# A planner with durations from a trace, and two fine levels of hgrn2 as products of VectorE summed by GpSimd

## The chip, the cores and the metric

The kernel runs on one core of one Trainium2 chip. The metric is the device time of one execution in microseconds. Beside it stands, for one profiled execution, the span from its first to its last instruction.

## The reference, cut to what matters

A hybrid block of two layers over 272 tokens (16 learned "meta" tokens and 256 of the input; the reference pads to 384 positions, of which the first 112 are masked), D = 1024. In each layer three branches, retention, hgrn2 and differential attention, read one projection of the normed input, are gated, added and projected back, and a feed-forward part with a convolution over three tokens (width 2816) follows.

```python
proj = hn @ w_in                                    # 1024 -> 13312
branches = jnp.stack([retention(...), hgrn2(...), diff_attention(...)], axis=2)
y = jnp.sum(jax.nn.sigmoid(mg) * einsum('blnc,ncd->blnd', branches, w_branch), axis=2)
h = h + y @ w_out
h = h + conv_ffn(rms_norm(h, norm_ffn_g[li]), ...)  # in both layers
...
# hgrn2, for each of 8 heads of 128 features and each chunk of 128 tokens:
cb  = jnp.cumsum(lfc, axis=1)                       # log of the forget gates f
dec = exp(cb[:, :, None] - cb[:, None, :])          # for keys up to the query, else 0
a = jnp.einsum('bqhd,bkhd,bqkhd->bhqk', qc, kc, dec)
o = jnp.einsum('bhqk,bkhe->bqhe', a, vc) + jnp.einsum('bqhd,bhde->bqhe', qc * jnp.exp(cb), state)
```

The decay between a query and a key is a product of forget gates, another for each feature, so `a` isn't a plain matrix product.

## The kernel before, in words

**The stream of weights.** Activations lie with the features on the 128 partitions and the tokens along the free axis. The matrices come as chunks of eight tiles of 128 x 128 (`wraw`, three buffers; `_Weights.next`). ScalarE rounds a chunk to fp32r (`whi`, four buffers), VectorE takes the remainder (`wlo` = `wraw` - `whi`, four buffers), and TensorE issues three fp32r matmuls for a tile: `whi` with the high part of x (`xh`; L915), `whi` with its low part (`xl`; L916), `wlo` with the high part (L917). They sum into `main` in PSUM. A matmul has 272 columns (tokens), in layer 1 mostly 258. The last product of layer 1 has its own loop (`fo`, L1429 to L1431).

**The order.** `ORDER` lists the projections of a layer in turn (`hq`, `hf`, ..., each with its tile pair). Marks among them place the work of the branches: at `+hga` the first four heads of hgrn2 can begin, at `!hga` they must be done, `hgb` is the second four. `products` records the stream and moves a clock on; `behind` and `settle` spread the operations of a branch between its two marks, as due times (`key`).

Nothing is issued while it is recorded. Each call on an engine goes through `_Engine.__getattr__`, which adds an operation with a cost, its operands and the due time to `_Plan` (hence all these instructions have one line, L607). `_Plan.order` is a list scheduler: it simulates the five engines with these costs, and each time takes, on the engine that comes free first, the operation that can start earliest, by due time among equals. `issue` then writes the instructions in the order found. So a cost that is changed anywhere can move instructions on every engine. Each engine's own queue runs in order on the chip.

**hgrn2 by levels.** `hg_heads(b)` does four heads; it is called for b = 0 (`hga`) and 1 (`hgb`) in each layer, four calls in all. `q` (tile `hq`), `k` (tile `hf`) and `total` (tile `he`, the forget gates) are 128 x 4 heads x 272 tokens. The pairs of a query and a key within a chunk of 128 tokens are divided by `LEVELS` = 64, 32, ..., 2, 1: level s holds those whose key lies in the left and whose query in the right half of one block of 2s tokens. The levels go from 1 up to 64. After each, the queries of right halves are multiplied by the total decay of the left half, the keys of left halves by that of the right half, and the totals of two blocks are multiplied into one (`tot`, seven steps of falling width; both products show as `hq<-hq,tot` and `hf<-hf,tot`, at level 1 with `he`), so that at the next level the decays already stand in `q` and `k`.

The scores of levels 1 to 16 lie within blocks of 32 tokens. For each of them `quarters` issues 32 small matmuls (4 heads x 2 chunks x 4 blocks, 32 keys by 32 or 16 queries) into a PSUM bank `lev` (L1107; the trace has two rows for each), and VectorE copies the wanted elements under a mask into `near` (`copy_predicated`; partitions: keys). The call for level 1 also takes the diagonal, the call for level 2 also pairs that are apart by a key and an odd query, from queries that ScalarE gathers in `extra` (name `odd`).

```python
if s == 1:
    quarters(wide, q, lambda hd, c, t: q[:, hd, tokens(c, t)])
    dve.copy_predicated(near, lev[:, 80:112].unsqueeze(1).to_broadcast([P, 8, 32]), wide)
elif s < 32:
    quarters(some..., q, lambda hd, c, t: right(q[:, hd : hd + 1, tokens(c, t)], s)[:, 0])
    fill(right(near, s), lev[:, 16 * (i - 2) : 16 * (i - 1)], some)
```

`hg_outputs` later multiplies the scores (`at`, which takes `near`) with the values.

**GpSimd** (POOL in the profile) copies halves of words for transposing DMAs (`apart`, `vt`, `tails`), clears tiles, multiplies in the norms, and sums over the partitions for the heads' norms: `partition_all_reduce`, `hr<-hsq`, over 272 columns. In an order it shows as ISA; a nameless ISA row there loads the code of such an operation.

Of the kernel before, what the change touches and what calls it, by code (L numbers as in the profile page):

```python
# [25 lines left out]
T = META + SEQ  # L26
# [9 lines left out]
LEVELS = (64, 32, 16, 8, 4, 2, 1)  # L36
# [232 lines left out]
def _constants():  # L269
# [40 lines left out]
    block = [level(s, 32, 16) for s in LEVELS[2:6]] + [odd(32, 16), even(32, 32)]  # L310
    lev[:, :112] = np.tile(np.concatenate(block, axis=1), (4, 1))
# [45 lines left out]
class _Plan:  # L357
# [96 lines left out]
    def order(self):  # L454
# [13 lines left out]
        later = {e: [] for e in engines}  # L468
        now = {e: [] for e in engines}
        count = 0  # L470
        tables = "le"
        beside = False

        def push(op):
# [29 lines left out]
        while len(out) < todo:  # L504
# [69 lines left out]
class _Engine:  # L574
# [5 lines left out]
    def __getattr__(self, method):  # L580
        f = getattr(self.engine, method)

        def call(*args, **kw):
            aps = [(k, x) for k, x in list(enumerate(args)) + list(kw.items()) if isinstance(x, bass.AP)]
            outs = [x for k, x in aps if k in (0, "out", "accum_out")]
            ins = [x for k, x in aps if k not in (0, "out", "accum_out")]
            n = math.prod(outs[0].shape[1:])
            cost = self.fixed + self.each * n
            if self.name == "act":
                cost += 0.093 * (len(aps) - 2) - (0.043 if ins[0].tensor.name in self.plan.psum else 0.0)  # L590
            elif self.name == "pool" and method != "memset":
                cost += 1.6e-3 * n
            if method == "partition_all_reduce":
                cost = 0.4 + 5.4e-3 * n
            if method == "reciprocal":
                cost += 7 * self.each * n
            elif method == "tensor_tensor_scan":
                cost += self.each * n
            elif method == "transpose":
                cost = 0.11  # L600
            elif method == "matmul" and args[1].dtype == F32R:
                cost = max(0.107, n / 2400 + 0.003)
            elif method == "matmul":
                cost = max(0.214 if args[1].shape[-1] > 32 else 0.07, 4 * n / 2400)
            elif method == "dma_start":
                cost = self.fixed + self.each * n * outs[0].shape[0]
            self.plan.add(self.name, lambda: f(*args, **kw), cost, outs, ins, args[2] if method == "activation" else None)  # L607

        return call

# [55 lines left out]

def _trace(ctx, tc, plan, a, depth, probe):
    nc = tc.nc
    act = _Engine(plan, nc.scalar, "act", 0.094, 0.833e-3)
    dve = _Engine(plan, nc.vector, "dve", 0.068, 1.042e-3)  # L670
    pe = _Engine(plan, nc.tensor, "pe", 0.0, 4 / 2400)
    pool = _Engine(plan, nc.gpsimd, "pool", 0.04, 0.85e-3)
    sync = _Engine(plan, nc.sync, "sp", 0.06, 4 / 360e3)
# [20 lines left out]
    def slot(name, dt=F32):  # L694
        return new(sp, [P, 4 * T], dt, "slot", SLOTS, name)
# [13 lines left out]
    def bank(name):  # L709
        return new(bp, [P, 512], F32, "bank", 2, name)  # L710
# [4 lines left out]
    def tt(out, x, y, op):  # L715
        dve.tensor_tensor(out=out, in0=x, in1=y, op=op)
# [175 lines left out]
    def products(xs, name, j, t0=0):  # L892
# [96 lines left out]
    for li in range(depth):  # L989
# [74 lines left out]
        def hg_heads(b):  # L1064
# [28 lines left out]
            def right(t, s):  # L1093
                return halves(t, s, t.shape[2])[:, :, :, 1, :]
# [22 lines left out]
            extra = slot("extra")  # L1117
            odd = extra[:, : 8 * P].rearrange("p (h c t) -> p h c t", h=4, c=2)
            act.activation(qt2[:, :, 8:], right(q[:, :, tail], 1)[:, :, :, 0], AF.Copy)
            act.activation(odd[:, :, :, 64:], q[:, :, : 2 * P].rearrange("p h (c n two) -> p h c n two", c=2, two=2)[:, :, :, :, 1], AF.Copy)  # L1120
            tt(right(q, 1), right(q, 1), right(total, 1), MUL)
            room, at0 = slot("tot"), 0
            for i, s in reversed(list(enumerate(LEVELS))):

                pl = bank("lev")
                wide = pl[:, :256].rearrange("p (g t) -> p g t", g=8)
                some = pl[:, :128].rearrange("p (g t) -> p g t", g=8)
                tokens = lambda c, t: slice(c * P + 32 * t, c * P + 32 * t + 32)  # L1130
                if s == 1:
                    quarters(wide, q, lambda hd, c, t: q[:, hd, tokens(c, t)])
                    dve.copy_predicated(near, lev[:, 80:112].unsqueeze(1).to_broadcast([P, 8, 32]), wide)
                elif s == 2:
                    act.activation(odd[:, :, :, :64].rearrange("p h c (n s) -> p h c n s", s=2),
                                   q[:, :, : 2 * P].rearrange("p h (c n two s) -> p h c n two s", c=2, two=2, s=2)[:, :, :, :, 1, :], AF.Copy)
                    quarters(wide.rearrange("p g (two t) -> p g two t", two=2), odd,
                             lambda hd, c, t: odd[:, hd, c, :].rearrange("p (two t) -> p two t", two=2)[:, :, 16 * t : 16 * t + 16])
# [258 lines left out]
        def final():  # L1397
# [15 lines left out]
            cost = 3 * (BANK / 2400 + 0.012)  # L1413
# [216 lines left out]
```

## Time and profile before

| | before |
|---|---|
| time, median of 3 runs | 1305.88 us (1304.24 to 1306.25) |
| the profiled execution | 1305.7 us, span 1303.9 us |
| mean granted TensorE clock | 0.998 |
| PE, matmuls | busy 1285.8 us, 99% of the span, 11678 instructions |
| PE, weight loads (PEld) | 1256.7 us, 96% |
| DVE (VectorE) | 986.7 us, 76%, 1589 instructions |
| ACT (ScalarE) | 786.7 us, 60%, 1282 instructions |
| POOL (GpSimd) | 270.3 us, 21%, 300 instructions |
| DMA | 225 MB, mean 173 GB/s |

A busy time is the time in which an engine had an instruction under way, and the shares are those of the whole span. In the groups of instructions a row has line, engine, operation, out<-in, tile shapes and count, then busy time and mean ns of one, then the engine's idle time ahead of them and what ended most of it. In the waits a row says who waited, for whom, how long in sum, how often, and the longest. Rows that begin with a time are single instructions or batches: start (us), duration, engine, line, operation, and in brackets an idle time just before them with what ended it. Rows that begin with two times are stretches of the span: its length, busy time (and count) of PE, PEld, DVE, ACT and POOL, then the granted clock, the DMA share and GB/s.

### The profile page before, as it was taken

What the parts mean: (1) busy time and instruction counts of PE and PEld (TensorE: products, weight loads), DVE (VectorE), ACT (ScalarE), POOL (GpSimd) and SP (SyncE); (2) the same over time, 40 slices, a digit from 0 to 9 for tenths busy, and PEclk for the clock granted to TensorE, in tenths of its full rate; (3) what the DMA queues carried; (4) which work ended last, traced back from release to release, by engine and by line L of the source; (5) the groups of instructions that cost most, each with busy time, mean ns of one, the idle gap of its engine ahead of it and who ended that gap; (6) DMA issues with size and microseconds to landing.
All of it is one profiled execution on the core that took longest, in us unless ns stands there. A gap on an engine that the chain in (4) does not pass through costs nothing.

```text
span 1303.9 us, 28637 instructions
## 1 busy us (share of the span) xinstructions
PE 1285.8 (99%) x11678; PEld 1256.7 (96%) x11678; DVE 986.7 (76%) x1589; ACT 786.7 (60%) x1282; POOL 270.3 (21%) x300
## 2 busy tenths in 40 slices
PE   9999999999999999999999999999999999999998
PEld 9999989999999999999999999899999999999986
DVE  7685897798686789886575768877986867898843
ACT  6746444746576567666456474447466765776643
POOL 5021262423422020000030212634223220200000
PEclk9999999999999999999999999999999999999999
DMA  7664665643744545555555646655446446466653
GB/s 272 200 179 147 173 178 155 164 160 125 199 138 157 182 156 178 183 173 183 175 178 185 186 149 185 179 155 168 159 138 199 145 162 198 144 207 196 201 190 112
DMA packets 86868, 225.36 MB, mean 173 GB/s; under 512 B 32976, under 2 KB 33104, under 8 KB 86736
## 3 DMA queue, kind: packets, MB, share of 16 engines
q1 hardware_dynamic: 86448, 223.00, 55.3%
q8 instruction: 92, 1.51, 0.5%
q10 hardware_dynamic: 288, 0.52, 0.1%
q14 instruction: 40, 0.33, 0.1%
HBM read 216.16 MB, written 1.05 MB: 167 GB/s over the span
## 4 chain that ended last, share of the span: by engine, by line
PE 88%; DVE 9%; issue 1%; ACT 1%; DMA 0%; SPq 0%; DVEq 0%; ACTq 0%
PE main L915 26%; PE main L917 26%; PE main L916 25%; DVE wlo L607 2%; PE fo L1430 2%; PE fo L1431 2%; PE fo L1429 2%; DVE two_b L607 1%; DVE two_a L607 1%; PE lev L1107 1%; PE ds L1291 1%; PE ho L607 1%; PE ro L607 1%; PE do L607 1%; DVE two_c L607 1%
## 5 line engine op out<-in xcount | busy, mean ns | idle before, releaser
L915 PE MATMUL main<-xh,whi 128*128 128x272 f32 (+1 forms) x2368 | 682.6, 288 | 0.8 <-ACT whi L607 0.8
L917 PE MATMUL main<-xh,wlo 128*128 128x272 f32 (+1 forms) x2368 | 673.9, 285 | 1.3 <-DVE wlo L607 0.7
L916 PE MATMUL main<-xl,whi 128*128 128x272 f32 (+1 forms) x2368 | 673.3, 284 | 1.5 <-DVE xl L607 1.5
L607 DVE TENSOR_TENSOR wlo<-wraw,whi 128x1024 fp32r<-128x1024 f32 (+1 forms) x411 | 512.0, 1250 | 187.8 <-ACT whi L607 186.6
L607 ACT ACTIVATE whi<-wraw 128x1024 fp32r<-128x1024 f32 (+1 forms) x411 | 427.5, 1042 | 250.9 <-PE main L916 166.3
L917 PEld LDWEIGHTS main<-xh,wlo 128*128 128x128 f32 x2368 | 446.5, 189 | 3.1 <-DVE wlo L607 2.3
L916 PEld LDWEIGHTS main<-xl,whi 128*128 128x128 f32 x2368 | 446.6, 189 | 2.2 <-DVE xl L607 1.9
L915 PEld LDWEIGHTS main<-xh,whi 128*128 128x128 f32 x2368 | 446.7, 189 | 2.0 <-ACT whi L607 1.0
L607 POOL TENSOR_TENSOR y<-h,rstd 128x272 f32<-128x272 f32 x32 | 34.6, 1112 | 318.1 <-ACT rstd L607 318.1
L607 POOL PARTITION_ALL_REDUCE hr<-hsq x36 | 65.8, 1837 | 88.9 <-ACT hsq L607 85.9
L607 DVE SCALAR_TENSOR_TENSOR two_b<-main,small,two_b 128x256 f32<-128x256 f32 (+2 forms) x144 | 65.3, 487 | 24.4 <-ACT two_b L607 22.7
L607 POOL COPY apart<-vsrc 128x512 uint16<-128x512 uint16 x48 | 40.7, 867 | 145.2 <-ACT vsrc L607 145.0
L607 ACT ACTIVATE two_b<-main,small 128x272 f32<-128x272 f32 (+1 forms) x72 | 37.3, 566 | 23.8 <-PE main L917 22.7
L915 PE MATMUL main<-ghi,whi 128*128 128x272 f32 x176 | 51.0, 290 | 0.0
L916 PE MATMUL main<-glo,whi 128*128 128x272 f32 x176 | 50.6, 287 | 0.0
L917 PE MATMUL main<-ghi,wlo 128*128 128x272 f32 x176 | 50.3, 286 | 0.0
L607 POOL COPY vt<-turned 128x512 uint16<-128x512 uint16 x32 | 37.0, 1160 | 29.2 <-DMA turned<-apart 29.0
L915 PE MATMUL main<-b0hi,whi 128*128 128x272 f32 (+1 forms) x128 | 37.9, 296 | 0.0
L915 PE MATMUL main<-b1hi,whi 128*128 128x272 f32 (+1 forms) x128 | 37.8, 296 | 0.0
L915 PE MATMUL main<-yhi,whi 128*128 128x272 f32 (+1 forms) x128 | 36.4, 284 | 0.0
L917 PE MATMUL main<-b0hi,wlo 128*128 128x272 f32 (+1 forms) x128 | 36.4, 284 | 0.0
L917 PE MATMUL main<-yhi,wlo 128*128 128x272 f32 (+1 forms) x128 | 36.3, 284 | 0.0
(235 smaller groups left out, 1970.1 us busy)
## 6 DMA issues: line engine op xcount, KB each, us to landing
wraw<-in_w SPq DMA_DIRECT2D x402, 512.0 KB, 3.4
h<-in_h SPq DMA_DIRECT2D x4, 272.0 KB, 5.1
dec<-in_dec SPq DMA_DIRECT2D x2, 544.0 KB, 4.9
wraw<-in_w SPq DMA_DIRECT2D x4, 256.0 KB, 4.2
const<-in_const SPq DMA_DIRECT2D x1, 937.0 KB, 5.6
turned<-apart SPq DMA_TRANSPOSE x48, 4.0
gain<-in_gl SPq DMA_DIRECT2D x1, 512.0 KB, 5.1
out<-y ACTq DMA_DIRECT2D x2, 256.0 KB, 2.8
```

Of the source, the lines that this page charges most:

```text
L607: self.plan.add(self.name, lambda: f(*args, **kw), cost, outs, ins, args[2] if method == "activation" else None)
L915: nc.tensor.matmul(o, wh, hi, start=first, stop=False)
L916: nc.tensor.matmul(o, wh, lo, start=False, stop=False)
L917: nc.tensor.matmul(o, wl, hi, start=False, stop=last)
L1107: nc.tensor.matmul(o, keys, x, start=True, stop=True)
L1291: nc.tensor.matmul(ss[m][:, at : at + nk], q[half, hd, q0 : q0 + P], k[half, hd, :nk], start=True, stop=True)
L1429: nc.tensor.matmul(o, gh, wh, start=False, stop=False)
L1430: nc.tensor.matmul(o, gl, wh, start=False, stop=False)
L1431: nc.tensor.matmul(o, gh, wl, start=False, stop=end)
```

## The change

It has two parts.

**The planner's costs.** ScalarE's and VectorE's fixed costs go up (0.094 to 0.2 us, 0.068 to 0.145), a main matmul's from 0.003 to 0.01 us over its columns, GpSimd's operations get costs of their own, a transposing DMA 0.7 us more. New is `RELOAD`: where GpSimd goes from a `tensor_tensor` to a `partition_all_reduce` or back, the plan adds 8 us.

**Levels 1 and 2 of `hg_heads`.** Instead of the groups of small matmuls VectorE forms products of a query and a key elementwise (128 features x all tokens of four heads), GpSimd sums them over the 128 partitions (`sums`: in pieces of 544 columns, five in a call), and VectorE copies from the sums in SBUF, 32 partitions at a time since each block of 32 tokens has its place there. `mine` is a query with its own key at odd tokens (before the decays), `prod` (1088 columns) both queries of a pair with the left key, and at level 2 the two queries of a right half with each of the two left keys (two halves of 544). ScalarE's two gathering copies are gone. There are two new slots of a shared pool, `prod` and `sums`, and the mask table has some other columns.

```diff
 class _Plan:
+    RELOAD = 8.0
...
+            if e == "pool" and op.func is not None:
+                if op.func != code:
+                    code, t = op.func, max(t, engines[e] + self.RELOAD)
...
+            elif self.name == "pool" and method == "tensor_tensor":
+                cost, kind = 0.55 + 2.1e-3 * n, method
+            elif method == "partition_all_reduce":
+                cost, kind = 0.2 + 6.3e-3 * n, method
...
-    act = _Engine(plan, nc.scalar, "act", 0.094, 0.833e-3)
-    dve = _Engine(plan, nc.vector, "dve", 0.068, 1.042e-3)
+    act = _Engine(plan, nc.scalar, "act", 0.2, 0.833e-3)
+    dve = _Engine(plan, nc.vector, "dve", 0.145, 1.052e-3)
...
-        cost = 3 * ((T - t0) / 2400 + 0.003)
+        cost = 3 * ((T - t0) / 2400 + 0.01)
...
+            def sums(out, prod):
+                for c in range(0, prod.shape[1], 2 * T):
+                    pool.partition_all_reduce(out[:, c : c + 2 * T], prod[:, c : c + 2 * T], P, ReduceOp.add)
...
-            act.activation(odd[:, :, :, 64:], q[...][:, :, :, :, 1], AF.Copy)
+            tt(mine, rows(q, 2)[:, :, 1], rows(k, 2)[:, :, 1], MUL)
+            sums(own, mine)
             tt(right(q, 1), right(q, 1), right(total, 1), MUL)
+            tt(prod.rearrange("p (n s) -> p n s", s=2), rows(q, 2), rows(k, 2)[:, :, 0:1].to_broadcast([P, 2 * T, 2]), MUL)
+            sums(total_of, prod)
+            for t, here in lanes():
+                dve.copy_predicated(blocks_of[here], lev[here, 80:112]..., by_chunk(total_of, P)[here, :, :, here])
+            for t, here in lanes():
+                dve.copy_predicated(blocks_of[here]...[:, :, :, :, 1], lev[here, 64:80]..., by_chunk(own, P // 2)[here, ...])
...
                 if s == 1:
-                    quarters(wide, q, lambda hd, c, t: q[:, hd, tokens(c, t)])
-                    dve.copy_predicated(near, lev[:, 80:112]..., wide)
+                    pass
                 elif s == 2:
-                    act.activation(odd[:, :, :, :64]..., q[...][:, :, :, :, 1, :], AF.Copy)
-                    quarters(wide..., odd, ...)
-                    fill(right(near, 2), lev[:, 48:64], wide[:, :, :16])
-                    fill(right(near, 1), lev[:, 64:80], wide[:, :, 16:])
+                    for kk, x in enumerate(halves_):
+                        tt(x.rearrange("p (n s) -> p n s", s=2), rows(q, 4)[:, :, 2:], rows(k, 4)[:, :, kk : kk + 1]..., MUL)
+                    sums(total_of, prod)
+                    for t, here in lanes():
+                        for kk, c in enumerate((48, 112)):
+                            dve.copy_predicated(to, split_s(mask), split_s(data))
```

The names in the rows that follow are tiles with a running number; the number tells which chunk or call a row belongs to.

VectorE in the second call of layer 0 (`hgb`), between the chunks `wlo_406` and `wlo_453`: `near_266` collects the scores, `hq_101_254` and `hf_44_149` are the call's queries and keys, `tot` its totals, `prod_268` the new products, `sums_269` and `extra_267` what GpSimd has summed. Before:

```order
L607 TENSOR_TENSOR wlo_406<-wraw_404,whi_405 128x1024
L607 COPY_PREDICATED near_266<-masks_80,lev_271 128x32x4
L607 TENSOR_TENSOR hq_101_254<-hq_101_254,tot_268 128x136x4
L607 TENSOR_TENSOR hf_44_149<-hf_44_149,tot_268 128x136x4
L607 TENSOR_TENSOR wlo_453<-wraw_451,whi_452 128x1024
```

And after:

```order
L615 TENSOR_TENSOR wlo_406<-wraw_404,whi_405 128x1024
L615 COPY_PREDICATED near_266<-masks_80,sums_269 32x256 x4
L615 COPY_PREDICATED near_266<-masks_80,extra_267 32x128 x4
L615 TENSOR_TENSOR prod_268<-hq_101_254,hf_44_149 128x544
L615 TENSOR_TENSOR hq_101_254<-hq_101_254,tot_270 128x272x2
L615 TENSOR_TENSOR hf_44_149<-hf_44_149,tot_270 128x272x2
L615 TENSOR_TENSOR wlo_453<-wraw_451,whi_452 128x1024
```

Three rows between two chunks became eleven, eight of them copies out of SBUF; the chain stands a level earlier at this place (level 2's decays, where level 4's stood).

VectorE in the first call of layer 0 (`hga`), behind `wlo_294`. Before:

```order
L607 TENSOR_TENSOR wlo_294<-wraw_292,whi_293 128x1024
L607 TENSOR_TENSOR hf_38_131<-hf_38_131,tot_217 128x4x8x16
L607 TENSOR_TENSOR hq_36_123<-hq_36_123,tot_217 128x4x8x16
L607 COPY_PREDICATED near_215<-masks_80,lev_222 128x8x16
L607 TENSOR_TENSOR wlo_298<-wraw_296,whi_297 128x1024
```

After (between the two pieces stand the other six `tot_219` steps, another `prod_217`, and level 2's `hf` and `hq`):

```order
L615 TENSOR_TENSOR wlo_294<-wraw_292,whi_293 128x1024
L615 TENSOR_TENSOR prod_217<-hq_36_123,hf_38_131 128x544
L615 TENSOR_TENSOR tot_219<-he_139 128x544
```
```order
L615 COPY_PREDICATED near_215<-masks_80,sums_218 32x256 x4
L615 COPY_PREDICATED near_215<-masks_80,extra_216 32x128 x2
L615 TENSOR_TENSOR hf_38_131<-hf_38_131,tot_219 128x136x4
L615 TENSOR_TENSOR hq_36_123<-hq_36_123,tot_219 128x136x4
L615 COPY_PREDICATED near_215<-masks_80,extra_216 32x128 x2
L615 TENSOR_TENSOR wlo_298<-wraw_296,whi_297 128x1024
```

Behind `wlo_294` the chain of levels was nearly done before; now it is at level 2, and 21 rows stand ahead of `wlo_298` instead of three.

GpSimd in that first call, ahead of the heads' norms (`hr<-hsq`). Before:

```order
L607 COPY vt_194<-turned_208 128x2x256 x2
L607 MEMSET am_265 128x64
L607 MEMSET near_266 128x256
L607 ISA
L607 ISA hr_233<-hsq_232 128x272
```

After:

```order
L615 COPY tails_195<-vsrc_196 128x32
L615 ISA
L615 ISA extra_216<-extra_216 128x544
L615 COPY vt_194<-turned_198 128x2x256 x2
L615 ISA sums_218<-prod_217 128x544 x2
L615 COPY apart_207<-vsrc_206 128x512 x2
L615 COPY tails_195<-vsrc_206 128x32
L615 MEMSET am_265 128x64
L615 ISA sums_218<-prod_217 128x544 x2
```

The code is loaded once, as before, but ahead of the sum of `mine`; five sums over 544 columns stand among the copies for the values.

TensorE in `hgb` of layer 0: where the first group of small matmuls stands in the stream (`main_380`, `main_400` and `main_450` are PSUM tiles of the stream). Before:

```order
L917 MATMUL main_380<-xh_16_91,wlo_383 128x272
L1107 MATMUL lev_269<-hq_101_254,hf_44_149 32x32 x32
L915 MATMUL main_380<-xh_16_91,whi_382 128x272
```

After:

```order
L925 MATMUL main_400<-xh_14_89,wlo_406 128x272
L1115 MATMUL lev_271<-hq_101_254,hf_44_149 32x16 x32
L615 MATMUL s_175_418<-rq_316,rk_333 128x272
L923 MATMUL main_450<-xh_16_91,whi_452 128x272
```

The first group of this call is now that of level 4 and stands five chunks later. Over the whole program TensorE has 576 calls of `lev` matmuls instead of 832 (1152 rows of the trace instead of 1664).

More of the change, by code (lines that the diff above doesn't have):

```diff
@@ L470, in order @@
         count = 0
-        tables = "le"
+        tables, code = "le", "tensor_tensor"
         beside = False
@@ L605, in call @@
             elif method == "dma_start":
-                cost = self.fixed + self.each * n * outs[0].shape[0]
-            self.plan.add(self.name, lambda: f(*args, **kw), cost, outs, ins, args[2] if method == "activation" else None)
+                cost = self.fixed + self.each * n * outs[0].shape[0] + (0.7 if kw.get("transpose") else 0.0)
+            self.plan.add(self.name, lambda: f(*args, **kw), cost, outs, ins, kind)
         return call
@@ L1119, in hg_heads, with by_chunk @@
+            def by_chunk(t, n):
+                return t.rearrange("p (h x) -> p h x", h=4)[:, :, : 2 * n].rearrange("p h (c x) -> p h c x", c=2)
+            extra, prod, total_of = slot("extra"), slot("prod"), slot("sums")
+            mine, own = extra[:, : 2 * T], extra[:, 2 * T :]
+            rows = lambda t, n: t.rearrange("p h (n s) -> p (h n) s", s=n)
             act.activation(qt2[:, :, 8:], right(q[:, :, tail], 1)[:, :, :, 0], AF.Copy)
-            act.activation(odd[:, :, :, 64:], q[:, :, : 2 * P].rearrange("p h (c n two) -> p h c n two", c=2, two=2)[:, :, :, :, 1], AF.Copy)
+            tt(mine, rows(q, 2)[:, :, 1], rows(k, 2)[:, :, 1], MUL)
@@ L1121, in hg_heads @@
+            sums(own, mine)
             tt(right(q, 1), right(q, 1), right(total, 1), MUL)
+            tt(prod.rearrange("p (n s) -> p n s", s=2), rows(q, 2), rows(k, 2)[:, :, 0:1].to_broadcast([P, 2 * T, 2]), MUL)
+            sums(total_of, prod)
+            blocks_of = near.rearrange("p (h c) t -> p h c t", c=2)
+            for t, here in lanes():
+                dve.copy_predicated(blocks_of[here], lev[here, 80:112].unsqueeze(1).unsqueeze(1).to_broadcast([32, 4, 2, 32]),
+                                    by_chunk(total_of, P)[here, :, :, here])
@@ L1122, in hg_heads @@
+            for t, here in lanes():
+                dve.copy_predicated(blocks_of[here].rearrange("p h c (n two) -> p h c n two", two=2)[:, :, :, :, 1],
+                                    lev[here, 64:80].unsqueeze(1).unsqueeze(1).to_broadcast([32, 4, 2, 16]),
+                                    by_chunk(own, P // 2)[here, :, :, 16 * t : 16 * t + 16])
             room, at0 = slot("tot"), 0
             for i, s in reversed(list(enumerate(LEVELS))):
-                pl = bank("lev")
-                wide = pl[:, :256].rearrange("p (g t) -> p g t", g=8)
@@ L1129, in hg_heads @@
-                some = pl[:, :128].rearrange("p (g t) -> p g t", g=8)
+                pl = bank("lev") if s > 2 else None
+                some = s > 2 and pl[:, :128].rearrange("p (g t) -> p g t", g=8)
                 tokens = lambda c, t: slice(c * P + 32 * t, c * P + 32 * t + 32)
                 if s == 1:
-                    quarters(wide, q, lambda hd, c, t: q[:, hd, tokens(c, t)])
-                    dve.copy_predicated(near, lev[:, 80:112].unsqueeze(1).to_broadcast([P, 8, 32]), wide)
+                    pass
@@ L1412, in final @@
                     pe.matmul(accs[t][k // 4][:, k % 4 * P : (k % 4 + 1) * P], h[:, k, tokens(t)], ident, is_transpose=True, start=k % 4 == 0, stop=False)
-            cost = 3 * (BANK / 2400 + 0.012)
+            cost = 3 * (BANK / 2400 + 0.0133)
             groups = [(t, c) for t in range(2) for c in range(2)]
```

36 lines of the change are left out of this document (19 added, 17 removed).

## The prediction

> **What bounds the kernel now.** I read the page first, then the waits, then stretches of the timeline.
>
> ```profile
> PE 1285.8 (99%) x11678; PEld 1256.7 (96%) x11678; DVE 986.7 (76%) x1589; ACT 786.7 (60%) x1282; POOL 270.3 (21%) x300
> PE 88%; DVE 9%; issue 1%; ACT 1%; DMA 0%; SPq 0%; DVEq 0%; ACTq 0%
> ```
>
> PE is the bound: it is never idle for long, and the chain that ended last runs through its weight stream. So a microsecond taken off PE's own work is a microsecond of the kernel, and so is each one for which PE has to wait. DVE, busy 76% on average, is off the path as long as its `wlo` tiles come in time. How much time it has is seen in the waits.
>
> ```profile
> DVE wlo L607 <- ACT whi L607: 186.6, 171, 4.7
> ACT whi L607 <- PE main L916: 166.3, 134, 2.9
> PE lev L1107 <- DVE hf L607: 3.2, 2, 1.7
> PE lev L1107 <- DVE tot L607: 0.4, 1, 0.4
> ```
>
> ACT waits for PE to free a `whi` buffer, DVE then for ACT: the split of the weights runs as far ahead as its four buffers let it, and no further. The small last rows are PE waiting for the hgrn2 chain. Here are the instructions that set the pace of both.
>
> ```profile
> 80.05 0.28 PE L917 MATMUL main<-xh,wlo 128*128 128x272 f32 x1
> 80.27 0.76 PE L1107 MATMUL lev<-hq,hf 128*32 128x32 f32 x64
> 80.96 0.40 PE L915 MATMUL main<-xh,whi 128*128 128x272 f32 x1
> 81.20 0.29 PE L916 MATMUL main<-xl,whi 128*128 128x272 f32 x1
> 81.33 0.29 PE L917 MATMUL main<-xh,wlo 128*128 128x272 f32 x1
> L607 ACT ACTIVATE whi<-wraw 128x1024 fp32r<-128x1024 f32 x399 | 421.4, 1057 | 246.1 <-PE main L916 163.2 <-PE fo L1430 26.5 <-DMA wraw<-in_w 26.3
> L607 DVE TENSOR_TENSOR wlo<-wraw,whi 128x1024 fp32r<-128x1024 f32 x399 | 504.3, 1268 | 184.2 <-ACT whi L607 183.1
> ```
>
> A main matmul starts 0.123 us after the one before (81.20 to 81.33 is 0.13, and the long stretches agree), so a chunk of eight weight tiles, 24 matmuls, lasts 2.95 us on PE. `whi` of a chunk can begin when PE is done with the chunk four before it, three chunks (8.85 us) ahead of its own use; less 1.06 for `whi`, 1.22 for an undisturbed `wlo` and some 0.3 for the handovers, a `wlo` is ready at most 6.2 us ahead. That lead is all that hides a burst of other work on DVE.
>
> **The change part by part.**
>
> *PE loses the 32-call groups of the two finest levels*, eight of them (two in each of four `hg_heads`). The rows from 80.05 to 81.33 span 1.28 us where three main matmuls would take 0.37: a group costs 0.91. **-7.3 us**, wholly on the path.
>
> *PE's waits in `lev`*: the two rows above are 3.6 us, and I take them as gone, since those groups now stand later: **-3.6**. One of them left more behind:
>
> ```profile
> 829.00:833.00 4.00, 2.30 (x75) 2.11 (x75) 3.96 (x7) 1.75 (x4) 3.96 (x5) 1.00 0.76 244
> 833.00:836.00 3.00, 3.00 (x40) 2.97 (x29) 3.00 (x5) 1.43 (x3) 1.06 (x1) 0.63 0.41 115
> 836.00:839.00 3.00, 3.00 (x79) 2.82 (x78) 1.16 (x3) 0.00 (x0) 0.54 (x1) 0.81 0.73 180
> ```
>
> PE idled 1.7 us before 833, and then the granted clock (third number from the end) was 0.63 and 0.81 for 3 us each: 1.1 + 0.6 = 1.7 us lost. **-1.7**, if the wait goes.
>
> *DVE gains work.* One call now has these rows more or dearer:
>
> ```profile
> L607 DVE TENSOR_TENSOR hf<-hf,tot 128x544 f32<-128x544 f32 x12 | 10.7, 894 | 0.2 <-PE lev L1107 0.2
> L607 DVE TENSOR_TENSOR hq<-hq,he 128x1088 f32<-128x1088 f32 x4 | 6.4, 1607 | 0.0
> L607 DVE COPY_PREDICATED near<-masks,lev 128x128 f32<-128x128 uint8 x20 | 7.0, 352 | 2.3 <-PE lev L1107 2.1
> L607 DVE COPY_PREDICATED near<-masks,lev 128x256 f32<-128x256 uint8 x4 | 1.8, 444 | 0.0
> L607 DVE TENSOR_TENSOR tot<-he 128x544 f32<-128x544 f32 x4 | 3.3, 818 | 0.0
> L607 DVE TENSOR_TENSOR tot<-tot 128x272 f32<-128x272 f32 x4 | 2.1, 516 | 0.1
> L607 DVE TENSOR_TENSOR tot<-tot 128x136 f32<-128x136 f32 x4 | 1.5, 373 | 0.1
> L607 DVE TENSOR_TENSOR tot<-tot 128x68 f32<-128x68 f32 x4 | 1.8, 448 | 0.1
> L607 DVE TENSOR_TENSOR tot<-tot 128x32 f32<-128x32 f32 x4 | 1.3, 335 | 0.1
> L607 DVE TENSOR_SCALAR he<-he,keep,floor 128x272 f32<-128x272 f32 x16 | 7.8, 518 | 0.0
> L607 DVE TENSOR_SCALAR hf<-hf,keep 128x272 f32<-128x272 f32 x16 | 7.6, 497 | 0.0
> ```
>
> Products: three of 544 elements (0.9 each) and one of 1088 (1.6), 4.3 us. Copies on 32 partitions: four of 256 elements (0.44) and twelve of 128 (0.35), 6.0; that a copy on a quarter of the partitions takes as long as one on all is my assumption, and the highest value. Gone are one of 256 and two of 128, 1.1. Net 9.2 us a call, 37 in all. Spread over 1304 us this would vanish; what counts is where it stands. I take the stretch in the second call of layer 0 (`hgb`), from the end of `wlo_386` to the end of `wlo_453`, five chunks later.
>
> After, DVE's rows there are seven TENSOR_TENSOR of 544 (6.3), two of 1088 (3.2), the first five `tot` steps (0.82 + 0.52 + 0.37 + 0.45 + 0.34 = 2.5), four copies of 256 and four of 128 (3.2) and five `wlo` (6.1): 21.3 us. Before, the same stretch held 17.5 (six of 544, one of 1088, `tot` of 544, 272, 136, 68, 32 and 16, one copy of 256, three of 128, five `wlo`). PE takes 5 x 2.95 = 14.75 us for the five chunks; before, four and a half `lev` groups stood among them (4.1); now all of these lie behind. `wlo_386` itself comes behind four `he` and four `hf` steps (4.1) and two short ones (0.9, both sides have them), so its lead is 6.2 + 2.95 - 4.1 - 0.9 - 1.2 = 2.95, and 4 if the `he` steps overlap as usual; I take 4. So the time to hand was 14.75 + 4.1 + 4 = 22.9 for 17.5, with 5 us to spare, and is now 18.8 for 21.3: **PE waits 2.5 us**. Layer 1 has the same rows between the same two `wlo`: another 2.5.
>
> In the first call (`hga`) the rows bunch instead: between `wlo_294` and `wlo_298` stand 11.7 us (six of 544, seven `tot` steps for 3.2, four and four copies) against 0.9 before. `wlo_298` ends 11.7 + 1.2 = 12.9 after `wlo_294`; it may take the lead of 6.2, a chunk of 2.95 and the `lev` group and transpose that follow (1.0), 10.2: a wait of 2.7. In layer 1 the bunch is 7.7 + 1.2 against 4.6 + 2.95 + 2.0 = 9.6: none. Sum of these waits: **+7.7**.
>
> *GpSimd gains 20 sums over 544 columns, and they hold DVE.* This is the cost that the plan doesn't know.
>
> ```profile
> 112.86 1.23 DVE L607 TENSOR_TENSOR wlo<-wraw,whi 128x1024 fp32r<-128x1024 f32 x1 [2.93 <-ACT whi L607]
> 114.90 3.79 POOL L607 PARTITION_ALL_REDUCE hr<-hsq  x2 [12.26 <-ACT hsq L607]
> 116.82 2.23 DVE L607 TENSOR_TENSOR wlo<-wraw,whi 128x1024 fp32r<-128x1024 f32 x1 [2.41 <-ACT whi L607]
> 158.06 1.88 POOL L607 PARTITION_ALL_REDUCE hr<-hsq  x1
> 159.70 1.22 DVE L607 TENSOR_TENSOR wlo<-wraw,whi 128x1024 fp32r<-128x1024 f32 x1 [1.69 <-ACT whi L607]
> ```
>
> The second sum of the pair began about 116.8. The `wlo` that began with it took 2.23 us instead of 1.23; the one that began in the last 0.24 us of a sum took 1.22. So the first part of a sum over 272 columns keeps an operation with two SBUF inputs waiting for 1.0 us. For 544 columns I estimate 2.0 (if it goes by columns; 1.0 if it goes by instructions) and a sum of 3.7. Nearly all of DVE's rows in the stretch above read two SBUF tiles, and DVE has no idle time there, so each of a call's five sums can add 0 (it falls on other rows) to 2.0 us: 0 to 10 for each `hgb`, 0 to 4 for `hga` of layer 0, 0 to 3.4 for `hga` of layer 1 (0.6 to spare), since there the first sums meet DVE with time to hand. I take three of five in `hgb` (6 + 6), one in `hga` of layer 0 (2) and 1 for layer 1: **+15**, of 0 to 27. Behind every wait stands a `wlo` in DVE's queue, and behind that PE.
>
> The Trainium skill ("GPSIMD Engine Reference", Specifications) states this contention for DVE instructions with two SBUF inputs or in a 2-port mode. By it the masked copies, which no row here shows beside a sum, would be held as well; the sum would then stand 4 us higher.
>
> *The cold clock again*: by the rows at 829 to 839, a wait of 1.7 us can cost another 1.7. Four places now wait longer than that, 6.8 us; a slower PE gives DVE time to catch up, so I count half: **+3.4**, of 0 to 6.8.
>
> The Trainium skill ("TensorE: Matmul & The Clock Gate", Part 1) has the clock halved only after about 3.4 us of idleness. The drop here came after 1.7, so the measurement decides; by the page the waits, which come in pieces, would leave the clock alone, and the forecast would be 3.4 lower.
>
> *At nothing*: ACT loses eight copies (busy 60%). GpSimd's change of code, the nameless row ahead of its first sum, was hidden before (that sum began 0.13 us after its `hsq`); now it stands right ahead of the first `extra` sum, but DVE asks for the result only behind `wlo_294`, some 18 us later, and the sums and copies between take 9.3: up to 9 us are covered, and the nearest row bounds it by the 12.3 us that GpSimd idled ahead of 114.90, so +3 at worst. *The new order elsewhere* (attention heads, feed-forward) I take at 0, -3 to +3: PE's other waits in the list are small.
>
> Sum: -7.3 - 3.6 - 1.7 + 7.7 + 15 + 3.4 = **+13.5 us**. The profiled execution took 1305.7 (its span is 1303.9), the median of the three runs is 1305.88: **1319 us**.
>
> **The rivals.** A measurement of this kernel can tell about 0.2% (2.6 us) from no change.
>
> *Faster, 20%*: the sums meet DVE while it waits or reads PSUM, and costs of copies are lower on 32 partitions. For it speaks that in most of the trace a `wlo` beside GpSimd takes its usual 1.22. Without any hold and cold clock: -12.6 + 7.7 = -4.9, 1301; if the leads cover the bunches too, -12.6, 1293. It decides where the waits added stay below 10 us.
>
> *No change that can be told, 12%*: the waits added come to 10 to 15 us.
>
> *Much slower, 18%*: every sum holds DVE for its 2 us, in all four calls: +27 instead of +15, with a cold clock each time: +29, 1335. GpSimd's own lateness would show here too: DVE's second product waits for GpSimd to have read the first, with the next `wlo` behind it.
>
> *Likeliest, 50%*: as summed.
>
> **How the numbers follow.** The forecast is 1319. The low end takes the hold-free case with a little of the bunching, 1298; the high end the full hold, 1335. Faster by over 0.2%: 0.20, within: 0.12, slower: 0.68 (0.50 + 0.18).
>
> **What the profile after would show.** Right: the `lev` rows of PE fall from 1664 to 1152; PE's idle time grows by some 15 to 20 us, ended by DVE `wlo` or `near`, near 105 us, 175 to 190 us and the same places of layer 1; the sums over 544 columns take 3.4 to 4 us; DVE's 544 rows beside them take 2 us longer; several dips of the granted clock. Wrong: PE without new waits at these places, or waits elsewhere.

## The result

The changed kernel took 1353.63 us (median of 4 runs, 1350.37 to 1354.72) against 1305.75 of the kernel before on the same chip: 47.9 us slower, a ratio of 1.036 (95% interval 1.0343 to 1.0377). The forecast was 13.5 us slower: it had the sign, and the hold of VectorE as its largest term, but little more than a quarter of the size.

The page of the changed kernel, first the engines, then the chain that ended last by engine:

```profile
PE 1296.6 (96%) x11166; PEld 1266.1 (94%) x11166; DVE 1066.6 (79%) x1657; ACT 777.0 (57%) x1270; POOL 346.3 (26%) x320
PE 74%; DVE 18%; issue 2%; DMA 2%; ACT 2%; POOL 2%; SPq 0%; DVEq 0%; ACTq 0%; POOLq 0%
```

The span is 1351.8 us, the mean granted clock 0.985 (before 1303.9 and 0.998). TensorE has 512 instructions less, as planned, and yet is busy 10.8 us longer. It is idle 55.2 us (1351.8 - 1296.6) where it was idle 18.1: 37.1 more. Both together are the 47.9. VectorE has doubled its share of the chain.

What TensorE waited for in the changed kernel (in all, times, longest):

```profile
PE main L925 <- DVE wlo L615: 17.9, 9, 7.1
PE lev L1115 <- DVE hq L615: 11.7, 4, 4.9
PE lev L1115 <- DVE hf L615: 6.7, 2, 3.8
```

The longest of these waits begins at 183 us, in `hgb` of layer 0. VectorE and GpSimd there, in order of time:

```profile
179.10 3.93 POOL L615 PARTITION_ALL_REDUCE extra<-extra  x1 [1.82 <-DVE extra L615]
179.80 3.36 DVE L615 TENSOR_TENSOR prod<-hq,hf 128x1088 f32<-128x1088 f32 x1
183.26 0.73 DVE L615 TENSOR_TENSOR hf<-hf,he 128x544 f32<-128x544 f32 x1
183.32 7.33 POOL L615 PARTITION_ALL_REDUCE sums<-prod  x2 [0.29 <-DVE prod L615]
183.90 3.47 DVE L615 TENSOR_TENSOR hq<-hq,he 128x1088 f32<-128x1088 f32 x1
187.30 5.08 DVE L615 TENSOR_TENSOR wlo<-wraw,whi 128x1024 fp32r<-128x1024 f32 x2
```

Three sums stand nearly back to back, and whatever VectorE issues within the first two microseconds of one gets to work only when that part is over: the product of 1088 takes 3.36 us and `hq` 3.47 (the shortest rows of these kinds take 1.6 and 1.3), and the two `wlo` 5.08 where two undisturbed ones take 2.4. The row of 544 that had begun 0.06 us before a sum kept its 0.73; there the sum became longer instead (3.9 us instead of 3.5). TensorE needs the first `wlo` from 183.6 on. In stretches of 3 us (length, then busy time and count of PE, PEld, DVE, ACT, POOL, then the granted clock, DMA share, GB/s):

```profile
180.00:183.00 3.00, 3.00 (x27) 3.00 (x26) 3.00 (x1) 0.06 (x1) 3.00 (x1) 1.00 0.32 124
183.00:186.00 3.00, 0.62 (x5) 0.40 (x4) 2.90 (x3) 1.20 (x2) 2.71 (x2) 1.00 0.00 0
186.00:189.00 3.00, 0.00 (x0) 0.00 (x0) 3.00 (x2) 0.74 (x2) 3.00 (x2) 0.69 0.00 0
189.00:192.00 3.00, 1.24 (x5) 1.24 (x6) 3.00 (x2) 0.00 (x0) 3.00 (x3) 0.50 0.16 22
192.00:195.00 3.00, 3.00 (x19) 3.00 (x18) 3.00 (x4) 0.00 (x0) 3.00 (x4) 0.68 0.78 235
195.00:198.00 3.00, 3.00 (x26) 3.00 (x25) 2.82 (x6) 1.96 (x2) 0.70 (x1) 1.00 0.70 273
```

TensorE stood from 183.6 to 190.8. The clock fell to half at about 187.1 (0.69 over 186 to 189) and was full again at 193.9 (0.68 over 192 to 195), so the first 3.2 us of work after the wait ran at half speed.

### The profile page after: what moved, and what is told of

It is laid out like the page before. It is cut to its first block, busy times and chain, and to the rows that moved or that the text cites. A ratio compares the mean times of both kernels' runs of the same rounds, so it can differ in the third digit from the quotient of the medians.

```text
span 1351.8 us, 27644 instructions
## 1 busy us (share of the span) xinstructions
PE 1296.6 (96%) x11166; PEld 1266.1 (94%) x11166; DVE 1066.6 (79%) x1657; ACT 777.0 (57%) x1270; POOL 346.3 (26%) x320
## 4 chain that ended last, share of the span: by engine, by line
PE 74%; DVE 18%; issue 2%; DMA 2%; ACT 2%; POOL 2%; SPq 0%; DVEq 0%; ACTq 0%; POOLq 0%
PE main L923 22%; PE main L925 21%; PE main L924 21%; DVE wlo L615 6%; DVE near L615 2%; DMA wraw<-in_w 2%; DVE hq L615 2%; PE fo L1467 1%; PE fo L1465 1%; PE fo L1466 1%; DVE hf L615 1%; DVE two_c L615 1%; ACT whi L615 1%; PE ds L1327 1%; DVE prod L615 1%
## 5 line engine op out<-in xcount | busy, mean ns | idle before, releaser
L615 DVE TENSOR_TENSOR wlo<-wraw,whi 128x1024 fp32r<-128x1024 f32 (+1 forms) x411 | 526.1, 1290 | 163.3 <-ACT whi L615 162.2
L925 PEld LDWEIGHTS main<-xh,wlo 128*128 128x128 f32 x2368 | 451.2, 191 | 18.7 <-DVE wlo L615 18.7
L924 PEld LDWEIGHTS main<-xl,whi 128*128 128x128 f32 x2368 | 451.7, 191 | 4.3 <-DVE xl L615 3.9
L923 PEld LDWEIGHTS main<-xh,whi 128*128 128x128 f32 x2368 | 452.2, 191 | 2.3 <-PE main L925 0.8
L615 POOL PARTITION_ALL_REDUCE hr<-hsq x36 | 73.0, 2043 | 101.0 <-ACT hsq L615 101.0
L615 POOL PARTITION_ALL_REDUCE sums<-prod x16 | 58.8, 3709 | 21.8 <-DVE near L615 19.2
L923 PE MATMUL main<-yhi,whi 128*128 128x272 f32 (+1 forms) x128 | 36.4, 284 | 0.0
L925 PE MATMUL main<-yhi,wlo 128*128 128x272 f32 (+1 forms) x128 | 36.4, 284 | 0.0
```

The costliest lines, as they stand in the source:

```text
L923: nc.tensor.matmul(o, wh, hi, start=first, stop=False)
L924: nc.tensor.matmul(o, wh, lo, start=False, stop=False)
L925: nc.tensor.matmul(o, wl, hi, start=False, stop=last)
```

## The experiments

Four theories. A: each sum over 544 columns holds VectorE for about 2 us, wherever it meets it. B: VectorE waits for what GpSimd has summed. C: the new order itself costs the time. D: VectorE's products and copies alone are too much. How long VectorE was held is counted in all runs in one way: of each VectorE row that overlaps a partition sum, what it took beyond the shortest row of its form. In the changed kernel that comes to 41.3 us beside the 20 sums, 2.06 each, and none of the four calls is spared.

**The new costs alone**, with the levels as before (`_Plan`, `_Engine` and the two matmul costs of the change, `hg_heads` and the masks of before).

> New planner costs with the old levels (small matmuls, copies from PSUM), so no sum over 544 columns. Theory A (each sum over 544 columns holds VectorE for about 2.1 us, VectorE falls behind with wlo, TensorE waits and its clock falls): the loss is not in the planner; 1300 to 1312 us. Theory C (the new order itself costs the time): 1335 us or more. TensorE's waits of over 0.5 us sum to 10 to 20 us by A, to 40 by C.

1315.21 us, a ratio of 1.0079 (1.0064 to 1.0094): 10.4 us slower. So neither A nor C alone: some of the loss comes with the costs, but not most. New among TensorE's waits is one for GpSimd's `tails`:

```profile
PE vm L614 <- POOL tails L614: 6.2, 3, 2.5
PE lev L1114 <- DVE hf L614: 4.6, 3, 2.2
```

**Which of the costs.** Two runs took one half each.

> The kernel before with GpSimd's new costs, RELOAD and the dearer transposing DMA alone. The planner's part cost 10 us. If that comes from here (TensorE's waits for the tails at the vm products, up to 2.8 us, point to GpSimd): 1311 to 1317 us; if from the other costs: 1303 to 1307 us.

> The kernel before with the new costs of ScalarE, VectorE and the main matmuls alone. If these carry the planner's 10 us: 1311 to 1317 us; if GpSimd's do: 1303 to 1307 us.

1311.69 us (1.0051, 1.0038 to 1.0063) and 1309.62 (1.0036, 1.0022 to 1.0049): +6.2 and +4.1, together about the 10.4. Both halves carry it: the first time lies in the range for GpSimd's half, the second between its two ranges. The pointer from the `vm` wait to GpSimd's half was wrong: the waits at `vm` (4.2 us in all, the longest 2.4) stand in the run with the other half, and in GpSimd's they are 0.4 in all.

**No wait for the sums, and shorter sums.** Three kernels in the changed kernel's order. The planner is told the same costs and tiles; the chip gets other operands.

```diff
-  pool.partition_all_reduce(out[:, c : c + 2 * T], prod[:, c : c + 2 * T], P, ReduceOp.add)
+  pool.partition_all_reduce(out[:, c : c + N], prod[:, c : c + N], P, ReduceOp.add)   # N = 544, 272, 32
-  dve.copy_predicated(to, mask, <from the sums>)
+  dve.copy_predicated(to, mask, <the same columns of q>)
```

> The changed kernel, same order; the masked copies of the two levels take their data from the queries' tile instead of the sums (so that part of the scores is left out), and so wait for no sum; the sums over 544 columns still run. A (the hold): as the changed kernel, 1346 to 1356 us. Theory B (VectorE waits for the results of GpSimd): 1310 to 1325 us.

> As the kernels with sums over 544 and 32 columns and no wait for them (1354.8 and 1322.7 us), with 272 columns. If the hold goes by columns, each is about 1.05 us and the time half way: 1334 to 1343 us. If VectorE's lead absorbs a short hold: 1323 to 1331 us. If a sum holds by the instruction: 1348 us or more.

> As the one before, and each of the 20 sums covers only 32 of its 544 columns (the rest of the scores of the two levels is left out); the order is that of the changed kernel. A: the hold is gone, and most of the loss with it, 1305 to 1320 us, no wait of TensorE over 4 us, clock above 0.993. B: no less than the kernel before it in this list, within 5 us. C: 1335 us or more. Theory D (VectorE's products and copies alone are too much): 1325 to 1335 us.

1354.78, 1335.87 and 1322.69 us. With full sums that nobody waits for, the time is that of the changed kernel, within 1.2 us: B falls. From 544 to 32 columns it drops by 32.1 us, and 272 columns lie between, 13.2 above the 32. VectorE was held for 42.7, 17.2 and 2.3 us: the hold goes by columns, and each microsecond of it above the 2.3 costs 0.8 to 0.9 us of time. TensorE's waits for `wlo`, with 544 columns and with 32:

```profile
PE main L925 <- DVE wlo L615: 17.7, 9, 7.1
...
PE main L925 <- DVE wlo L615: 4.1, 7, 1.1
```

Shorter sums also take less of GpSimd's time, but that isn't what helped: TensorE's waits for GpSimd's `tails` are 4.3 us with 544 columns and 4.9 with 32. With 32 columns there is next to no hold, and still 18 us over the kernel before remain: more than A allowed and less than D's range, 1325 to 1335.

TensorE's instructions are the same and in the same order in these runs, so their traces can be set side by side, instruction by instruction. In the profiled executions the full width of the sums costs 7.6 us in the first call (`hga` of layer 0), 9.5 in `hgb`, and 7.5 and 9.8 in layer 1; elsewhere it costs less than 1 us.

**Each sum twice**, by a second call of the same sum.

> The changed kernel with each of the 20 sums issued twice in a row; the planner counts it once, the order is the same. A: 20 more holds of 2.1 us, all in stretches where VectorE is already late: 1385 to 1410 us, and VectorE's rows beside the sums are longer by 42 us in all. B: DVE waits 3.5 us longer for each of the results that it needs at once, at most eight of them: 1360 to 1380 us. C and D: within 10 us of the changed kernel.

1396.42 us: 42.8 more. VectorE was held for 75.9 us instead of 41.3, 34.6 more and not the 42 expected. So the time rose by 8 us more than the holds: here GpSimd is late as well (TensorE waits 10.8 us for `tails` instead of 3.9, VectorE 3.5 once for a sum), and this run alone doesn't give the price of a hold. The sums themselves run one behind the other at the same price:

```profile
L1134 POOL PARTITION_ALL_REDUCE sums<-prod x32 | 118.5, 3726 | 11.3 <-DVE near L615 9.8
```

**The copies, and what is left without them.** The kernel with 32 columns once without the masked copies, then also without products and sums, so that only the order is left; and the one with 544 columns without the copies.

```diff
-  plan.add("dve", lambda: nc.vector.copy_predicated(to, mask, data), ...)
+  plan.add("dve", lambda: None, ...)            # the cost and the place in the plan stay
```

> The kernel with sums over 32 columns and no wait for them (1322.7 us), without the masked copies of the two levels (24 in a call, some 10 us of VectorE a call; that part of the scores is left out). If what remains of the loss is VectorE's added work: 1308 to 1316 us. If it is the order (small matmuls that stand ahead of main matmuls and wait for the chain of levels): 1319 to 1324 us.

> The same order once more, without the products, sums and copies of the two levels (all of that part of the scores is left out). Left are the planner's new order and the 7.3 us of small matmuls less on TensorE. With new costs alone the time was 1315.2 us, so if the order made for the products costs nothing of its own: 1305 to 1311 us. If it does: 1312 us or more.

> The changed kernel in its own order with the sums over 544 columns, without the 16 masked copies of each call (7 us of VectorE a call; that part of the scores is left out). Without copies and with sums over 32 columns the time was 1302.6 us. If copies and holds compete for the same room of VectorE, the 41 us of holds now find 28 us more of it: 1308 to 1324 us. If each hold costs by itself, wherever VectorE stands: 1330 to 1338 us, 32 us more, as between 1322.7 and 1354.8.

1302.59, 1300.44 and 1331.02 us, the first two below every range that was expected. (There are 16 copies in a call, not the 24 of the first text.) The copies cost 20.1 us beside short sums and 23.8 beside full ones; full sums cost 28.4 without copies and 32.1 with them. The two prices add, with 3.7 us on top where both are there: no common reserve of VectorE had covered a part of one. The rows of the copies, with short sums, and below them TensorE's waits in that kernel:

```profile
L1155 DVE COPY_PREDICATED near<-masks,hq 32x128 f32<-32x128 uint8 x48 | 23.6, 492 | 1.1
L1155 DVE COPY_PREDICATED near<-masks,hq 32x256 f32<-32x256 uint8 x16 | 7.9, 495 | 0.4
```
```profile
PE lev L1115 <- DVE near L615: 9.1, 4, 3.6
PE lev L1115 <- DVE hf L615: 2.5, 2, 1.4
```

Both rows of waits are absent without the copies. The new copies stand in VectorE's queue ahead of the chain of levels and of the copies that empty the `lev` banks. TensorE's groups of small matmuls wait for these, and the stream of weights stands behind the groups in TensorE's own queue. One such place in the kernel with 32 columns:

```profile
198.60 3.72 DVE L1155 COPY_PREDICATED near<-masks,hq 32x128 f32<-32x128 uint8 x7
202.35 0.30 DVE L615 COPY_PREDICATED near<-masks,lev 128x128 f32<-128x128 uint8 x1
202.80 0.73 PE L1115 MATMUL lev<-hq,hf 128*32 128x16 f32 x64 [3.65 <-DVE near L615]
```

TensorE's busy time tells the rest; the four kernels have the same instructions and order there (sums over 32 columns with copies, without, the order alone; then 544 columns without copies):

```profile
PE 1286.8 (97%) x11166; PEld 1257.5 (95%) x11166; DVE 1026.1 (78%) x1657; ACT 776.2 (59%) x1270; POOL 296.2 (22%) x320
...
PE 1279.9 (98%) x11166; PEld 1252.0 (96%) x11166; DVE 994.7 (77%) x1593; ACT 776.1 (60%) x1270; POOL 296.2 (23%) x320
...
PE 1279.0 (99%) x11166; PEld 1251.6 (96%) x11166; DVE 979.6 (75%) x1577; ACT 776.2 (60%) x1270; POOL 270.5 (21%) x300
...
PE 1288.9 (97%) x11166; PEld 1260.6 (95%) x11166; DVE 1035.5 (78%) x1593; ACT 776.7 (58%) x1270; POOL 351.5 (26%) x320
```

The changed kernel's 1296.6 is 17.6 above the 1279.0 of the bare order, for the same instructions. Of this 14.6 us are lost to the clock that the waits have lowered: TensorE works at half of it for 32.6 us there and for 3.4 in the bare order. What makes the other 3 us isn't shown. Of the 20.1 us of the copies 6.9 are such longer busy time, the rest is idle time.

**The hold in the plan.** The planner takes VectorE's time for each sum.

```diff
             engines[e] = t + cost
+            if e == "pool" and op.func == "partition_all_reduce":
+                engines["dve"] = max(engines["dve"], t + 0.58 * cost)
```

> The changed kernel, and the planner now counts VectorE as taken for 0.58 of the cost of each partition sum (2.1 us of one over 544 columns, 1.1 of one over 272). If the loss comes from the plan not knowing of the hold, so that wlo stands behind held rows: 1320 to 1340 us. If VectorE simply has no room for 41 us of holds in these stretches, wherever they are put: 1345 to 1360 us.

1387.11 us: worse by 33 than the changed kernel, which neither side expected. VectorE was held 36.4 us there, hardly less. What grew are TensorE's waits for the chain:

```profile
PE lev L1117 <- DVE hf L617: 20.6, 4, 9.3
PE lev L1117 <- DVE near L617: 19.6, 2, 9.9
PE main L927 <- DVE wlo L617: 13.2, 9, 4.9
```

In `hga` of layer 0 VectorE now idles for the sums, and then has the chain in one piece:

```profile
93.84 2.91 DVE L617 TENSOR_TENSOR prod<-hq,hf 128x544 f32<-128x544 f32 x1 [8.97 <-POOL sums L617]
...
112.40 4.14 DVE L617 COPY_PREDICATED near<-masks,sums 32x128 f32<-32x128 uint8 x8
116.57 0.62 DVE L617 COPY_PREDICATED near<-masks,lev 128x128 f32<-128x128 uint8 x2
117.01 1.06 PE L1117 MATMUL lev<-hq,hf 128*32 128x16 f32 x64 [9.66 <-DVE near L617]
```

Why the list scheduler puts TensorE's groups so early there stays open. The edit also takes more than the hold: where GpSimd changes its code, ahead of the first sum of `hga` in each layer, the plan's start of the sum lies `RELOAD`'s 8 us later, and VectorE counts as taken until then too. So the run doesn't show what a plan with the holds alone would do.

**The same in the plan of the kernel before**, for its heads' sums alone.

> The kernel before with its own costs, and the planner counts VectorE as taken for 0.58 of the cost of each of the heads' sums over 272 columns (1.1 us). Holds there add 18 us to VectorE in all, but TensorE waits only 13 us in all in this kernel, little of it beside these sums: 1302 to 1308 us; a gain of over 3 us would say that unknown holds cost the kernel before time, too.

1302.76 us, a ratio of 0.9982 (0.9974 to 0.9991): 2.7 us, or 0.2%, faster than before, about the bound of what can be told, and the only version that computes everything and is faster than both. VectorE's hold beside the heads' sums fell from 15.8 to 12.7 us; whether the gain is that, or just another order, isn't separated.

**The same sums elsewhere.** The kernel before with spare sums in the feed-forward part; the orders of TensorE, VectorE and ScalarE are unchanged. First 20 of a resident tile, then 22 that each read what a pair of products has just written.

```diff
+  pool.partition_all_reduce(<temp>, h[:, :2, :]..., P, ReduceOp.add)                        # 20, layer 0
---
+  pool.partition_all_reduce(<temp>, st["ghi"][j // 4][:, j % 4 - 1 : j % 4 + 1, :]..., ...)  # 22, odd j
```

> The kernel before with 20 further sums over 544 columns of a resident tile, results unused, one for each pair of feed-forward products of layer 0, where VectorE is busy about 68%; the orders of TensorE, VectorE and ScalarE are word for word those of before. If a hold costs only where VectorE has no lead left: 1303 to 1309 us, although VectorE's rows beside the sums are 30 to 42 us longer in all. If a hold costs wherever it falls: 1325 us or more.

> The kernel before with 22 further partition sums (544 columns in layer 0, 512 in layer 1), results unused, one behind every second pair of feed-forward products, so one in about 12 us; each reads what that pair has just written. The orders of TensorE, VectorE and ScalarE are word for word those of before. In the run with 20 such sums back to back VectorE was never idle for 70 us, and each hold went into the time. If a hold costs nothing where VectorE has time to make it good before the next: 1303 to 1310 us. If the place doesn't matter: 1330 us or more.

1338.44 us (1.0249, 1.0234 to 1.0264) and 1313.97 (1.0062, 1.005 to 1.0075). The first 20 didn't come one per pair: nothing held them back, and 19 of them ran back to back from 498 to 569 us. They held VectorE for 33.1 us, and the time rose by 32.5. The 22 paced ones held it for 39.1 us, and the time rose by 8.2. The same stretches, first with the sums back to back, then paced; last the second one in the kernel before:

```profile
500.00:520.00 20.00, 11.69 (x71) 10.90 (x70) 20.00 (x22) 5.75 (x11) 19.53 (x6) 0.87 0.19 61
520.00:560.00 40.00, 31.21 (x229) 29.81 (x228) 39.93 (x38) 18.40 (x30) 38.99 (x12) 0.96 0.39 132
```
```profile
500.00:520.00 20.00, 18.59 (x147) 18.28 (x148) 19.93 (x29) 11.92 (x20) 7.19 (x2) 1.00 0.54 179
520.00:560.00 40.00, 40.00 (x326) 40.00 (x326) 39.65 (x57) 26.33 (x43) 11.11 (x3) 1.00 0.59 181
```
```profile
520.00:560.00 40.00, 40.00 (x327) 40.00 (x326) 32.54 (x55) 26.77 (x41) 0.00 (x0) 1.00 0.57 183
```

VectorE is full with the sums in both; before it had 7.5 us of 40 to spare. With three sums in 40 us TensorE never waits; with twelve it stands for 9 of 40. So a hold costs its full length where VectorE can't make it good before the next, and about a fifth of it at one in 12 us. The 32 us in `hg_heads` fit this, as the holds fell there into stretches where VectorE had nothing left.

## Why the prediction was wrong

The ladder of the runs, in the changed kernel's own order: the order alone is 5.5 us faster than before; the products with sums over 32 columns add 2.2; the copies 20.1; the full width of the sums 32.1; waiting for them takes nothing (-1.2, within the spread of the runs). Sum 47.7.

Set beside the prediction's sum, with TensorE's longer busy time taken out of each step and counted as the clock:

| step | predicted | measured |
|---|---|---|
| TensorE's own work, its `lev` waits, the new order | -12.6 | -5.5 |
| products and copies | +7.7 | +14.5 |
| the hold | +15 | +22.4 |
| the clock | +3.4 | +17.5 |
| waiting for the sums | none | -1.2 |

So all four terms were set too low, the clock by most. It goes back to the steps ahead of it: TensorE has more and longer waits than the prediction found, because it let too few sums hold VectorE and left TensorE's small matmuls out of those who wait for it.

- **TensorE's own work and its waits in `lev`** (-7.3, -3.6, -1.7): the work is right, the busy time of the bare order is 6.8 us below that of before. The waits aren't. In the bare order none in `lev` is left, but its idle time is 19.3 us against 18.1 (4.1 of it for `tails`), and it has a stretch at half clock as before. In the changed kernel the `lev` waits come to 19.9 us.
- **The new order elsewhere, "at 0, -3 to +3"**: wrong. -12.6 became -5.5, so the order cost 7.1; with the old levels the new costs alone cost 10.4.
- **The hold, "+15, of 0 to 27"**: the mechanism and the size of one were right (2.0 us and 3.7 for a sum were estimated; 2.06 on average and 3.4 to 4.4 measured). The step that failed is the count: three of five in `hgb` and one in `hga` were taken to meet VectorE. Nearly all did, 41.3 us. Most was missed in `hga`, where the prediction let VectorE's time to hand cover the first sums: there the full width costs 7.6 and 7.5 us, clock included, for the 2 and 1 of the sum; in `hgb` 9.5 and 9.8 for 6 and 6. In a stretch where VectorE has no idle time, a sum can't miss it: this followed from the prediction's own sentence on that stretch. And the copies, which the prediction names but leaves out of its sum, are held too, as two rows of the changed kernel show:

```profile
199.97 3.76 DVE L615 COPY_PREDICATED near<-masks,extra 32x128 f32<-32x128 uint8 x4
200.03 3.50 POOL L615 PARTITION_ALL_REDUCE sums<-prod  x1 [4.33 <-DVE near L615]
```

  Four copies take 1.8 us alone (0.44 each); here one of them waited 1.95. The Trainium skill ("GPSIMD Engine Reference", Specifications) had this rule, and the trace agrees.
- **Products and copies, +7.7**: 22.3 with the clock, 14.5 without. A copy on a quarter of the partitions took 0.49 us on average at 128 and at 256 elements (0.35 and 0.44 were taken), 31.5 us in all. But the failed step is another: the working counted what `wlo` can wait and not the chain. With short sums the copies add 13.1 us to TensorE's idle time, and its `lev` waits, none without the copies, are 11.9 there: its small matmuls wait for `hf` and `hq` or for a copy that empties their bank, and have no buffer ahead.
- **The clock, +3.4, of 0 to 6.8**: 17.5 us of longer busy time, spread over the terms above (9.7 of the 32.1 and 7.8 of the 22.3). The prediction counted four waits that are long enough, and half their price; the trace has nine idle times of TensorE of over 1.5 us where before had one, and seven stretches at half clock, of 3.4 or 6.8 us, where before had one.
- **GpSimd's change of code, at nothing**: right, as far as the runs show. Without a wait for any sum the time is the same.
- **The rivals**: "much slower" came true with its mechanism, every sum holding, and was given 18% and 1335 us. It lacked the copies' chain and the clock of all the waits.
- **The signs**: the new waits stand where they were expected (108 to 113 and 184 to 191 us, and at the same places of layer 1), but TensorE's idle time grew by 37.1 us, not by 15 to 20.

## What to carry to other kernels

Before work is moved to GpSimd, look at what VectorE does beside it: a partition sum held VectorE's operations with two inputs in SBUF for more than half of its own length (2.3 of 3.5 us at 544 columns), and no row of VectorE's says so except by being longer than its kind. Price this at full length where VectorE's rows follow one another without a gap, and at little where it has time to recover. And count a burst on VectorE against every consumer in TensorE's queue: the weights had 6 us of lead here by the prediction's working, the small matmuls of the chain next to none.

## What the runs showed of the hardware

- The hold is the first part of a partition sum, about 2.3 us of 3.5 at 544 columns, 1.0 of 1.9 at 272. It met operations with two SBUF inputs and masked copies in SBUF; rows that read PSUM (`two_b<-main` beside the spare sums, 0.48 us as always) weren't held. A row under way when the sum began kept its time, and the sum took longer (3.9 to 4.4 instead of 3.5).
- The clock was halved 3.5 us after TensorE's last matmul at 183.6 and full 3.2 us after the work went on. The Trainium skill ("TensorE: Matmul & The Clock Gate", Part 1) gives about 3.4 us for both; at this place the trace agrees. The other six stretches at half clock in the changed kernel don't follow it: over all seven the clock was halved 2.2 to 4.6 us after the last matmul and full 3.2 to 6.3 us after the work went on. One followed a wait of only 2.4 us, at 1038 us (granted clock 0.57 over 1040 to 1044), and the one in the kernel before a wait of 1.7. There the measurement decides.
